# The blocks of an expert in turned order on odd steps, 64 slots for the expert of rank 24, and another pairing of the experts

## The chip, the cores and the metric

The kernel runs on one core of a Trainium2 chip. The core has five engines with a queue of instructions each: PE (TensorE, matrix multiplies), DVE (VectorE), ACT (ScalarE), POOL (GpSimd) and SP (SyncE, which starts transfers). The metric is the device time of one execution in microseconds; all times here are microseconds unless they are marked ns.

## The reference

One layer of a decoder for 1024 tokens of width 1024. Its last part, which the change touches, sends each token to 4 of 32 experts and adds up what these give, weighted:

```
act = clamped_swiglu(xb @ w_up[e] + b_up[e])     # w_up[e]: 1024 x 2048
return act @ w_down[e] + b_down[e]               # w_down[e]: 1024 x 1024
...
return jnp.zeros_like(h).at[slot_tok].add(ys * slot_gate[:, None].astype(ys.dtype))
```

Here `xb` are the tokens of one expert. The output of this part is added to its input and normalised. Ahead of it stand the projections, a sliding-window attention, a convolution branch, a layer norm and the router. All is float32.

## The kernel before, in words

The first 663 us are everything up to the router; then the experts run, and a short tail adds the result, normalises and stores it.

**Slots and blocks.** The experts are ranked by their number of tokens, and the one of rank j has `CAPS[j]` slots; what goes beyond them is done by a loop at the end, `overflow`, which runs no expert when all fit. The tokens of an expert are cut into blocks of 128, 64 or 32: 160 slots are 128 + 32, 320 are 128 + 128 + 64, 96 are 64 + 32. A block of 128 uses the whole array of PE; of 64 two column groups, of 32 four, with plain float32 matmuls. An expert with a block of 128 is `split`: each weight tile is cut into a high half (ACT, L87) and a low half (DVE, L88), and a 128-wide block takes three matmuls for each half of the outputs (L252). The narrower blocks use the weight tile as it came (L261).

**Steps and pairs.** An expert has 12 steps, each for one piece of weights: steps 0 to 3 make the first half of the up projection, 4 to 7 the second, 8 to 11 the down projection. In each step, `mm` runs over the expert's blocks, in rising order. Two experts make a pair (`PAIRS`, by rank) and take turns, four steps each; the pairs run one after the other, and the two experts of the last pair one after the other. Names in the trace begin with the rank: `p13l` is a low half of a weight tile of the expert of rank 13, `p13u` its accumulator of the up projection, `p13d` that of the down projection.

**What is issued around the matmuls.** Step numbers g run over the whole stage. A table, filled by `at(g, function, ...)`, says what is issued behind the matmuls of step g: the splits of weights, up to six halves ahead of the step that uses them; the transposes of a block's input (`x_T`); behind an expert's steps 3 and 7 the activation of all its blocks (`swiglus`, DVE L271 to L277 and ACT); the transposes of the activations (`act_T`); behind step 11 the evacuation of the result, scaled by the gates (`scale_out`, ACT L316); two steps later the scatter (`scatter`, POOL L320), an indirect transfer for each block that adds rows to `yd` in memory, one waiting for the landing of the one before. The bias of a 128-wide block comes by POOL: a row is loaded (L211), and broadcast to all partitions (`bias_of`, L226). Each engine runs its queue in the order of issue. There are five accumulators, handed out in the order in which they came free. The count of overflowing tokens, some 25 small operations on DVE, stands behind step 200.

Of the kernel before, what the change touches and what calls it, by code (L numbers as in the profile page):

```python
# [49 lines left out]
BROW, BC, ACTB, XG = 2, 3, 3, 3  # L50
V_AT, S_AT = (2, 3, 4, 5, 7), (0, 3)
CAPS = [320, 288, 256, 256, 256, 256, 192, 192, 192, 160, 160, 160, 160, 128, 128, 128,
        128, 128, 128, 96, 96, 96, 96, 96, 96, 64, 64, 64, 64, 64, 64, 64]
PAIRS = [(6, 31), (1, 30), (13, 19), (2, 29), (9, 14), (7, 20), (21, 22), (0, 28), (15, 23), (3, 27), (10, 16), (8, 24),
         (11, 17), (4, 26), (12, 18), (5, 25)]
TR = 9 * P
FDVE = (0, 4)

# [2 lines left out]
def kernel(ctx: ExitStack, tc: tile.TileContext, x, w_in, b_in, attn_sinks, w_attn_br,  # L61
# [33 lines left out]
    def acc(name):  # L95
        return ps.tile([P, 512], F32, name=name, tag="acc", bufs=5)
# [4 lines left out]
    class Expert:  # L101
# [130 lines left out]
        def mm(self, s, before=None):  # L232
            if s < 8 and s % 4 == 0 or s == 8:
                self.acc = [[acc(f"{self.pfx}{'d' if s == 8 else 'u'}{s}{i}{h}") for h in range(2 if w == P else 1)]
                            for i, (w, c) in enumerate(self.blocks)]
            raw, hi, lo = self.raw.pop(s), self.hi.pop(s, None), self.lo.pop(s, None)
            for i, (w, c) in enumerate(self.blocks):
                if before:
                    before(i)
                lhs = self.x[i] if s < 8 else self.aT[i]  # L240
                ng = P // w
                for kk in range(2):
                    k = 2 * (s % 4) + kk if s < 8 else 2 * (s - 8) + kk
                    st, sp = k == 0, k == KC - 1
                    if w == P and self.split:
                        terms = [(lhs[0], hi[kk]), (lhs[0], lo[kk]), (lhs[1], hi[kk])]
                    else:
                        terms = [(lhs[0], raw[kk])]
                    if w == P:
                        for h in range(2):  # L250
                            for j, (a, b) in enumerate(terms):
                                nc.tensor.matmul(self.acc[i][h], a[:, k, :], b[:, h * 512:(h + 1) * 512],  # L252
                                                 start=st and j == 0, stop=sp and j == len(terms) - 1)
                    else:
                        for j, (a, b) in enumerate(terms):
                            for g in range(ng):
                                if s < 8 and w == 32:
                                    rhs = b.rearrange("p (a f b t) -> p a b f t", a=2, b=2, t=2)[:, g // 2, g % 2]
                                else:
                                    rhs = b[:, g * 8 * w:(g + 1) * 8 * w]  # L260
                                nc.tensor.matmul(self.acc[i][0][g * w:(g + 1) * w, :8 * w], a[:, k, :], rhs,  # L261
                                                 start=st and j == 0, stop=sp and j == len(terms) - 1)
            wfree.extend(self.held.pop(s))
# [14 lines left out]
                                           op1=ALU.mult)  # L278

        def swiglus(self, v):  # L280
            for i, (w, c) in enumerate(self.blocks):
                for h in range(2 if w == P else 1):
                    self.swiglu(v, i, h)

# [41 lines left out]
    with ExitStack() as dctx:  # L326
# [391 lines left out]
        for b in range(NB + 1):  # L718
            i = 8 + b
# [119 lines left out]
        for c in range(KC):  # L839
            i = 38 + c  # L840
# [53 lines left out]
        for c in sorted(set(CAPS)):  # L894
            i, n = CAPS.index(c), CAPS.count(c)
# [198 lines left out]
        def expert_of(j):  # L1094
            ev = {}

            def value(eng=None):
                key = gated[0], eng
                if key not in ev:
                    src = (ids, ids2)[gated[0]]  # L1100
                    ev[key] = (eng or nc.sync).value_load(src[0:1, j:j + 1], min_val=0, max_val=NE - 1)
                return ev[key]

            return Expert(f"p{j}", CAPS[j], value, [t[:, j] for t in IDX])

        ex = [expert_of(j) for pair in PAIRS for j in pair]

# [71 lines left out]
    with tc.manual_schedule():  # L1179
# [173 lines left out]
        def at(g, f, *a):  # L1353
            todo.setdefault(g, []).append((f, a))
# [4 lines left out]
        for n, e in enumerate(ex):  # L1359
            p = g0[e.pfx] // 24 * 24  # L1360
            if n > 1:
                at(p - 16, e.fetch)
                at(p - 13, e.indices)
            for v in range(2):
                q = pos[e.pfx, 4 * v]
                at(q - 4, e.load_bias, v)
                at(q - 4, e.load_row, 2 * v)
                at(q - 3, e.load_row, 2 * v + 1)
                at(q, e.bias_of, 2 * v)
                at(q + 1, e.bias_of, 2 * v + 1)  # L1370
                at(q + 3, e.swiglus, v)
            for i in range(e.nb):
                at(pos[e.pfx, 4 + i], e.act_T, 0, i)
                at(pos[e.pfx, 8 + (i > 0)], e.act_T, 1, i)
                if e is not last:
                    at(pos[e.pfx, 11], e.scale_out, i)
            if e is not last:
                at(pos[e.pfx, 11] + (0 if e is ex[-2] else 2), e.scatter)
# [32 lines left out]
        e = ex[0]  # L1411
# [19 lines left out]
    with tc.If(nxv > 0):  # L1431
        last.scatter()
        with tc.For_i(0, nxv, 1) as it:
# [5 lines left out]
            e = Expert("x", P, lambda eng=nc.sync: ev[eng], idx, fast=False)  # L1439
# [48 lines left out]
```

## Time and profile before

| | |
|---|---|
| median of 3 runs | 2171.82 (2171.25 to 2172.2) |
| profiled execution | 2172.18, its span 2170.6 |
| busy: PE, DVE, ACT, POOL | 2065.7 (95%), 1373.6 (63%), 887.2 (41%), 487.9 (22%) |
| PE's granted clock, mean | 0.981 |
| moved by DMA | 508.74 MB, 234 GB/s |

Busy time of the engines overlaps, since they work beside each other; an engine with 95% bounds the kernel in most of the stretches, but not in each. The granted clock is a share of full speed.

### The profile page before, as it was taken

What the parts mean: (1) busy time and instruction counts of PE and PEld (TensorE: products, weight loads), DVE (VectorE), ACT (ScalarE), POOL (GpSimd) and SP (SyncE); (2) the same over time, 40 slices, a digit from 0 to 9 for tenths busy, and PEclk for the clock granted to TensorE, in tenths of its full rate; (3) what the DMA queues carried; (4) which work ended last, traced back from release to release, by engine and by line L of the source; (5) the groups of instructions that cost most, each with busy time, mean ns of one, the idle gap of its engine ahead of it and who ended that gap; (6) DMA issues with size and microseconds to landing.
All of it is one profiled execution on the core that took longest, in us unless ns stands there. A gap on an engine that the chain in (4) does not pass through costs nothing. (4 is left out here: it accounts for less than half of the span.)

```text
span 2170.6 us, 31922 instructions
## 1 busy us (share of the span) xinstructions
PE 2065.7 (95%) x10929; PEld 1368.4 (63%) x10929; DVE 1373.6 (63%) x2049; ACT 887.2 (41%) x1357; POOL 487.9 (22%) x649
## 2 busy tenths in 40 slices
PE   7999999998967999999999999999999999999993
PEld 6776788886744566566764346546766456767771
DVE  3768799666755545655965135465587559649755
ACT  3155511432333424444553122434366346446533
POOL 1000000004323221422322332133133332223111
PEclk9999999999988999999999999999999999999996
DMA  5111111142238988998898997799879988988985
GB/s 162 39 39 30 30 46 53 44 133 71 88 136 280 328 278 297 371 344 282 307 306 295 350 344 269 268 312 376 300 243 311 330 267 311 353 290 292 338 275 188
DMA packets 191302, 508.74 MB, mean 234 GB/s; under 512 B 34781, under 2 KB 71055, under 8 KB 191134
## 3 DMA queue, kind: packets, MB, share of 16 engines
q1 hardware_dynamic: 162342, 446.76, 58.0%
q0 software_dynamic: 28240, 58.23, 10.8%
q8 instruction: 87, 1.43, 0.3%
q10 hardware_dynamic: 551, 1.66, 0.2%
q14 instruction: 82, 0.66, 0.1%
HBM read 473.08 MB, written 33.49 MB: 233 GB/s over the span
## 5 line engine op out<-in xcount | busy, mean ns | idle before, releaser
L601 DVE SCALAR_TENSOR_TENSOR c<-a,cw,c 128x1024 f32<-128x1024 f32 x120 | 154.1, 1284 | 3.3
L829 POOL DMA_DIRECT2D bu<-in_b_up_dram x2 | 1.0, 502 | 450.8 <-DVE wol L88 450.8
L140 POOL DMA_DIRECT2D slt<-tab x103 | 54.4, 530 | 26.1 <-issue 12.9
L91 PE MATMUL ga<-xh,whga 128*128 128x512 f32 x128 | 52.1, 407 | 0.0
L93 PE MATMUL ga<-xh,wlga 128*128 128x512 f32 x128 | 50.5, 395 | 0.0
L92 PE MATMUL ga<-xl,whga 128*128 128x512 f32 x128 | 50.5, 394 | 0.0
L93 PE MATMUL gb<-xh,wlgb 128*128 128x512 f32 x128 | 50.4, 394 | 0.0
L91 PE MATMUL gb<-xh,whgb 128*128 128x512 f32 x128 | 50.4, 394 | 0.0
L92 PE MATMUL gb<-xl,whgb 128*128 128x512 f32 x128 | 50.4, 394 | 0.0
L1022 POOL DMA_INDIRECT tab<-rec,dst x32 | 32.4, 1011 | 59.5 <-DMA tab<-rec,dst 56.8
L928 PE MATMUL wo<-woh,mh 128*128 128x512 f32 x128 | 37.0, 422 | 0.6 <-ACT mh L87 0.6
L928 PE MATMUL wo<-woh,ml 128*128 128x512 f32 x128 | 35.9, 404 | 0.0
L88 DVE TENSOR_TENSOR p8l<-p8w,p8h 128x1024 fp32r<-128x1024 f32 x24 | 29.3, 1274 | 10.2 <-ACT p8h L87 6.1
L88 DVE TENSOR_TENSOR p7l<-p7w,p7h 128x1024 fp32r<-128x1024 f32 x24 | 29.5, 1279 | 9.7 <-ACT p7h L87 6.1
L442 ACT ACTIVATE gt<-ga,pcol 128x512 f32<-128x512 f32 x16 | 11.0, 691 | 59.2 <-PE ga L93 59.1
L88 DVE TENSOR_TENSOR p5l<-p5w,p5h 128x1024 fp32r<-128x1024 f32 x24 | 29.0, 1242 | 9.8 <-ACT p5h L87 9.2
L644 DVE SCALAR_TENSOR_TENSOR sc<-s,mask 128x512 f32<-128x512 f32 (+1 forms) x32 | 19.5, 652 | 23.9 <-PE s L641 21.8
L88 DVE TENSOR_TENSOR p0l<-p0w,p0h 128x1024 fp32r<-128x1024 f32 x24 | 29.5, 1266 | 7.5 <-ACT p0h L87 7.3
L928 PE MATMUL wo<-wol,mh 128*128 128x512 f32 x128 | 33.9, 399 | 0.0
L88 DVE TENSOR_TENSOR p11l<-p11w,p11h 128x1024 fp32r<-128x1024 f32 x24 | 29.3, 1275 | 4.8 <-ACT p11h L87 4.6
L88 DVE TENSOR_TENSOR p15l<-p15w,p15h 128x1024 fp32r<-128x1024 f32 x24 | 28.0, 1221 | 6.4 <-ACT p15h L87 6.1
L88 DVE TENSOR_TENSOR p1l<-p1w,p1h 128x1024 fp32r<-128x1024 f32 x24 | 28.5, 1240 | 5.0 <-ACT p1h L87 4.4
(1266 smaller groups left out, 6374.8 us busy)
## 6 DMA issues: line engine op xcount, KB each, us to landing
p6w<-in_w_up_dram SPq DMA_DIRECT2D x16, 512.0 KB
p31w<-in_w_up_dram SPq DMA_DIRECT2D x16, 512.0 KB
p1w<-in_w_up_dram SPq DMA_DIRECT2D x16, 512.0 KB
p30w<-in_w_up_dram SPq DMA_DIRECT2D x16, 512.0 KB
p13w<-in_w_up_dram SPq DMA_DIRECT2D x16, 512.0 KB
p19w<-in_w_up_dram SPq DMA_DIRECT2D x16, 512.0 KB
p2w<-in_w_up_dram SPq DMA_DIRECT2D x16, 512.0 KB
p29w<-in_w_up_dram SPq DMA_DIRECT2D x16, 512.0 KB
```

Source lines behind the costliest of these rows:

```text
L88: nc.vector.tensor_tensor(lo, src, hi.bitcast(F32), op=ALU.subtract)
L91: nc.tensor.matmul(o, ah, bh, start=start, stop=False)
L92: nc.tensor.matmul(o, ah, bl, start=False, stop=False)
L93: nc.tensor.matmul(o, al, bh, start=False, stop=stop)
L140: nc.gpsimd.dma_start(self.m[g * w:(g + 1) * w, i, :], tab[bass.ds(row + c, w), :])
L442: nc.scalar.activation(GT[c][:, sl], t, AF.Sigmoid, bias=bin_c(14 + c))
L601: nc.vector.scalar_tensor_tensor(C[c], A[c][:, w:w + S], cw[:, c, w:w + 1], C[c], op0=ALU.mult, op1=ALU.add)
L644: nc.vector.scalar_tensor_tensor(SC[b][c0 // 2][:, g::2, :W], t[g][:, :, :W], 0.125, mk[:, None, :].to_broadcast([P, 2, W]), op0=ALU.mult, ...
L829: nc.gpsimd.dma_start(bu, b_up[:, i * S:(i + 1) * S])
L928: nc.tensor.matmul(t, ml[:, k, :], W[k][:, sl], start=n == 0, stop=n == 3 * KC - 1)
L1022: nc.gpsimd.indirect_dma_start(out=tab[:, :], out_offset=bass.IndirectOffsetOnAxis(ap=DST[b][:, k:k + 1], axis=0), in_=REC[:, b, k, :], in ...
```

## The change

It has four parts: the expert of rank 24 has 64 slots instead of 96; the pairs are others; on odd steps `mm` runs over the blocks in falling order, so that the block that ended a step also begins the next; and the activations, the transposes of activations and the evacuations run over the blocks in falling order. The scatters keep the rising order.

```
 CAPS = [320, 288, 256, 256, 256, 256, 192, 192, 192, 160, 160, 160, 160, 128, 128, 128,
-        128, 128, 128, 96, 96, 96, 96, 96, 96, 64, 64, 64, 64, 64, 64, 64]
-PAIRS = [(6, 31), (1, 30), (13, 19), (2, 29), (9, 14), (7, 20), (21, 22), (0, 28), (15, 23), (3, 27), (10, 16), (8, 24),
-         (11, 17), (4, 26), (12, 18), (5, 25)]
+        128, 128, 128, 96, 96, 96, 96, 96, 64, 64, 64, 64, 64, 64, 64, 64]
+PAIRS = [(6, 31), (1, 30), (13, 14), (2, 29), (9, 19), (3, 28), (10, 20), (0, 27), (15, 16), (4, 26), (8, 23), (17, 18),
+         (11, 21), (7, 24), (12, 22), (5, 25)]
...
-            for i, (w, c) in enumerate(self.blocks):
+
+            for i in range(self.nb)[::-1 if s % 2 else 1]:
+                w, c = self.blocks[i]
...
         def swiglus(self, v):
-            for i, (w, c) in enumerate(self.blocks):
+            for i, (w, c) in reversed(list(enumerate(self.blocks))):
                 for h in range(2 if w == P else 1):
                     self.swiglu(v, i, h)
...
-            for i in range(e.nb):
+            for i in reversed(range(e.nb)):
                 at(pos[e.pfx, 4 + i], e.act_T, 0, i)
                 at(pos[e.pfx, 8 + (i > 0)], e.act_T, 1, i)
                 if e is not last:
```

Lines behind the change in `mm` have numbers that are higher by 2 in the changed kernel: L252 is L254, L261 is L263, L271 is L273, L316 is L318, L320 is L322.

**DVE at the start of the third pair.** That pair was (13, 19) and is (13, 14). What stands in DVE's queue around the first activation of expert 13 (`p13t`), before:

```order
L88 TENSOR_TENSOR p13l_6651<-p13w_6513,p13h_6650 128x1024
L88 TENSOR_TENSOR p13l_6694<-p13w_6515,p13h_6693 128x1024
L88 TENSOR_TENSOR p13l_6698<-p13w_6517,p13h_6697 128x1024
L271 TENSOR_TENSOR p13t_6780<-p13u_6654,p13bc_6683 128x512
L275 TENSOR_SCALAR p13t_6780<-p13t_6780 128x256
L276 SCALAR_TENSOR_TENSOR p13t_6780<-p13t_6780 128x256
L277 SCALAR_TENSOR_TENSOR p13act_6779<-p13sg_6782,p13t_6780 128x256
```

And in the changed kernel:

```order
L88 TENSOR_TENSOR p13l_6668<-p13w_6506,p13h_6667 128x1024
L88 TENSOR_TENSOR p13l_6672<-p13w_6508,p13h_6671 128x1024
L88 TENSOR_TENSOR p14xl_6692<-p14xt_6693,p14xh_6691 128x512
L88 TENSOR_TENSOR p14xl_6692<-p14xt_6700,p14xh_6691 128x512
L88 TENSOR_TENSOR p14l_6713<-p14w_6519,p14h_6712 128x1024
L88 TENSOR_TENSOR p14l_6717<-p14w_6521,p14h_6716 128x1024
L88 TENSOR_TENSOR p14l_6737<-p14w_6555,p14h_6736 128x1024
L88 TENSOR_TENSOR p14l_6741<-p14w_6557,p14h_6740 128x1024
L273 TENSOR_TENSOR p13t_6761<-p13u_6645,p13bc_6663 128x512
L277 TENSOR_SCALAR p13t_6761<-p13t_6761 128x256
L278 SCALAR_TENSOR_TENSOR p13t_6761<-p13t_6761 128x256
L279 SCALAR_TENSOR_TENSOR p13act_6760<-p13sg_6763,p13t_6761 128x256
```

The low halves of expert 14's input and of its first two steps have come to stand between expert 13's last halves of that phase and its activation; expert 19 needed none.

**ACT at the end of the second pair.** The evacuations of expert 1 (blocks 0 and 1 of 128, block 2 of 32 slots; `slt` holds the gates), before:

```order
L316 ACTIVATE p1ys0_6576<-p1d800_6360,slt_3627 128x512
L316 ACTIVATE p1ys0_6576<-p1d801_6361,slt_3627 128x512
L316 ACTIVATE p1ys1_6579<-p1d810_6362,slt_3627 128x512
L316 ACTIVATE p1ys1_6579<-p1d811_6363,slt_3627 128x512
L316 ACTIVATE p1ys2_6582<-p1d820_6364,slt_3627 128x256
```

And in the changed kernel:

```order
L318 ACTIVATE p1ys2_6567<-p1d820_6355,slt_3627 128x256
L318 ACTIVATE p1ys1_6569<-p1d810_6353,slt_3627 128x512
L318 ACTIVATE p1ys1_6569<-p1d811_6354,slt_3627 128x512
L318 ACTIVATE p1ys0_6572<-p1d800_6351,slt_3627 128x512
L318 ACTIVATE p1ys0_6572<-p1d801_6352,slt_3627 128x512
```

Block 0 has moved from the first place to the last. In POOL's queue of the changed kernel, where `gi` and `si` are the row numbers that a scatter writes to, these stand behind them:

```order
216 L211 DMA p13br0_6584<-bud128_69 1x16x32
217 L322 DMA yd_68<-p1ys0_6572,gi_3628 1152x1024
218 L322 DMA yd_68<-p1ys1_6569,gi_3628 1152x1024
219 L322 DMA yd_68<-p1ys2_6567,si_3629 4608x256
...
221 L211 DMA p13br1_6609<-bud128_69 1x16x32
222 L226 ISA p13bc0_6663<-p13br0_6584 128x512
...
225 L226 ISA p13bc1_6707<-p13br1_6609 128x512
```

Their order is that of the kernel before: the scatter of block 0 first, and the broadcasts of expert 13's two bias rows behind all three.

**PE between two steps of a 160-slot expert.** Expert 9, from the end of its step 0 to the beginning of its step 1, before (the numbers in the accumulators' names end in block and half):

```order
L252 MATMUL p9u001_8165<-p9h01_8134,p9xl0_8085 128x512
L261 MATMUL p9u010_8166<-p9w00_7946,p9xr1_8115 32x256 x4
L261 MATMUL p9u010_8166<-p9w01_7948,p9xr1_8115 32x256 x4
L252 MATMUL p9u000_8164<-p9h10_8142,p9xh0_8084 128x512
L252 MATMUL p9u000_8164<-p9l10_8143,p9xh0_8084 128x512
```

And in the changed kernel:

```order
L254 MATMUL p9u001_8251<-p9h01_8220,p9xl0_8169 128x512
L263 MATMUL p9u010_8252<-p9w00_8030,p9xr1_8201 32x256 x4
L263 MATMUL p9u010_8252<-p9w01_8032,p9xr1_8201 32x256 x4
L166 MATMUL p19xt00_8278<-ident_60,p19xg0_7947 128x64 x8
L263 MATMUL p9u010_8252<-p9w10_8073,p9xr1_8201 32x256 x4
L263 MATMUL p9u010_8252<-p9w11_8075,p9xr1_8201 32x256 x4
L254 MATMUL p9u000_8250<-p9h10_8228,p9xh0_8168 128x512
```

The narrow block of step 1 now follows that of step 0, here with transposes of the partner's input between them, and the 128-wide block comes behind it.

## Rows read from the trace of the kernel before

**Rows 1.** Windows by pair: PE, PEld, DVE, ACT, POOL busy; clock; DMA; GB/s

```profile
857.70:932.10 74.40, 74.15 (x480) 42.01 (x478) 47.92 (x68) 35.02 (x50) 25.96 (x36) 1.00 1.03 363
...
1024.90:1113.60 88.70, 86.65 (x524) 62.15 (x523) 81.39 (x104) 58.39 (x75) 27.00 (x35) 1.00 0.88 296
...
1403.80:1487.50 83.70, 77.48 (x484) 43.77 (x482) 53.10 (x103) 34.91 (x50) 25.20 (x35) 0.96 0.96 330
...
1580.30:1671.30 91.00, 88.20 (x525) 63.21 (x524) 81.04 (x104) 58.51 (x75) 34.92 (x36) 0.98 0.89 296
```

**Rows 2.** Timeline of PE: start, length; narrow blocks of ranks 30, 24, 11

```profile
854.13 3.65 PE L261 MATMUL p30d<-p30w,p30ar 128*64 128x512 f32 x16
...
1681.43 0.68 PE L166 MATMUL p24xt<-ident,p24xg 32*128 32x32 f32 x8
...
1691.65 11.67 PE L261 MATMUL p24u<-p24w,p24xr 128*64 128x512 f32 x96
...
1771.92 1.11 PE L261 MATMUL p11u<-p11w,p11xr 128*32 128x256 f32 x16
```

**Rows 3.** Timeline of PE: a 64-wide block of expert 8 between 128-wide ones

```profile
1716.03 0.39 PE L252 MATMUL p8u<-p8l,p8xh 128*128 128x512 f32 x1
1716.25 0.39 PE L252 MATMUL p8u<-p8h,p8xl 128*128 128x512 f32 x1
1716.57 1.94 PE L261 MATMUL p8u<-p8w,p8xr 128*64 128x512 f32 x8
1718.44 0.50 PE L252 MATMUL p8u<-p8h,p8xh 128*128 128x512 f32 x1
1718.78 0.40 PE L252 MATMUL p8u<-p8l,p8xh 128*128 128x512 f32 x1
```

**Rows 4.** Groups of PE, pair (10, 16), transposes: busy, mean ns, idle

```profile
L297 PE MATMUL p16aT<-ident,p16act 128*128 128x128 f32 x8 | 1.3, 281 | 0.0
...
L166 PE MATMUL p16xt<-ident,p16xg 128*128 128x128 f32 x8 | 1.1, 279 | 0.0
```

**Rows 5.** Timeline of DVE, start of pair (13, 19); in brackets idle, releaser

```profile
855.86 6.90 DVE L88 TENSOR_TENSOR p13l<-p13w,p13h 128x1024 fp32r<-128x1024 f32 x6
...
870.46 0.69 DVE L271 TENSOR_TENSOR p13t<-p13u,p13bc 128x512 f32<-128x512 f32 x1 [5.10 <-POOL p13bc L226]
...
876.26 0.69 DVE L271 TENSOR_TENSOR p13t<-p13u,p13bc 128x512 f32<-128x512 f32 x1 [3.78 <-POOL p13bc L226]
```

**Rows 6.** Timeline of POOL: first scatter of expert 1

```profile
846.30 1.67 POOL L320 DMA_INDIRECT yd<-p1ys,gi  x1 [21.15 <-ACT p1ys L316]
```

**Rows 7.** Timeline of ACT: evacuations of expert 1

```profile
844.63 1.38 ACT L316 ACTIVATE p1ys<-p1d,slt 128x512 f32<-128x512 f32 x2 [8.10 <-PE p1d L252]
...
849.07 0.47 ACT L316 ACTIVATE p1ys<-p1d,slt 128x256 f32<-128x256 f32 x1 [0.34 <-PE p1d L261]
```

**Rows 8.** Timeline of DVE, pair (10, 16)

```profile
1601.94 4.63 DVE L88 TENSOR_TENSOR p16l<-p16w,p16h 128x1024 fp32r<-128x1024 f32 x4 [0.41 <-ACT p16h L87]
...
1648.20 0.69 DVE L88 TENSOR_TENSOR p10al<-p10aT,p10ah 128x512 fp32r<-128x512 f32 x1
```

**Rows 9.** Timeline of DVE, pair (15, 23): overflow count, its first, what follows

```profile
1435.29 0.18 DVE L1231 TENSOR_TENSOR over<-scnt_ps,capr 128x32 f32<-128x32 f32 x1
...
1441.74 0.69 DVE L88 TENSOR_TENSOR p15al<-p15aT,p15ah 128x512 fp32r<-128x512 f32 x1
```

**Rows 10.** Timeline of PE, pair (15, 23): a matmul behind a gap

```profile
1443.61 0.79 PE L252 MATMUL p15u<-p15l,p15xh 128*128 128x512 f32 x1 [5.39 <-DVE p15l L88]
```

**Rows 11.** Timeline of all engines: end of expert 5 and the gather behind it

```profile
2104.25 1.37 ACT L316 ACTIVATE p5ys<-p5d,slt 128x512 f32<-128x512 f32 x2 [6.93 <-PE p5d L252]
2105.91 1.69 POOL L320 DMA_INDIRECT yd<-p5ys,gi  x1 [19.00 <-ACT p5ys L316]
...
2106.97 1.37 ACT L316 ACTIVATE p5ys<-p5d,slt 128x512 f32<-128x512 f32 x2 [1.35 <-PE p5d L252]
...
2123.19 1.02 POOL L1287 DMA_INDIRECT yg<-yd,si  x1 [3.74 <-DMA yd<-p5ys,gi]
```

## The prediction

> **What bounds the kernel now.** I first cut the trace into stretches of one pair each, from one pair's first matmul to the next pair's [rows 1]. The four pairs of a 160-slot and a 128-slot expert and the pair of 128 and 96 slots show two kinds of bound. In all of them PE is busy nearly throughout; in the 160+128 pairs DVE is busy too, 81 to 82 of 89 to 91 us, since every 128-wide block makes it form the low half of each weight tile. In pairs with one such expert DVE is busy about 50 us. So the expert stage is bound by PE, with DVE close behind wherever two split experts meet. The last 40 us are a chain of scatter, load, statistics and output.
>
> **What PE no longer does: 14.5 us.** Expert 24 loses its 32-wide block. Four of its steps (64 + 32) take 11.67, two steps of a 64-slot expert 3.65, so four take 7.2 [rows 2]: 4.5 in each of three phases, 13.5; then eight transposes of its input, 0.68, and two of its activations, estimated at 0.3 from those. In the reference's draw that expert (25th by its count) has 57 tokens, so 64 slots hold them and the overflow loop stays empty; had it more than 64, that loop would run a whole expert for it.
>
> **Changes of form: 12 us.** Turning the order on odd steps makes blocks of one width neighbours across a step's end. Counted in PE's listing, the expert matmuls change between 128-, 64- and 32-wide 382 times before and 241 times after. Of the 141, 21 are expert 24's own, counted above; 120 are left. The price, from one 64-wide block between two 128-wide ones [rows 3]: matmuls follow each other by 0.23, the last before the change takes 0.32, the first after the block 0.34, and the block 1.87 against 1.82 alone [rows 2]. That is 0.09 + 0.05 + 0.11 for a change there and one back, some 0.12 each; 0.09 if only one side pays, 0.17 if the last matmul of the narrow block waits too. A third of the places have transposes between the steps, which change the form anyway, so I take 0.10: 12 us, bounds 11 and 20. [...]
>
> **Old stalls that go: 24 us.** A 128-wide block's step is 12 x 0.23 = 2.74, and one with a 32-wide block 2.74 + 1.11 + 0.15 = 4.0 [rows 2, 3]. A 160+128 pair needs 12 x (4.0 + 2.74) = 81. Its transposes take 1.1 for the input and 1.3 for the activations of each 128-wide block [rows 4], with the narrow block and the changes of form around them about 5: 86. The four such pairs took 88.7 to 91.0 [rows 1], the two not shown 88.9 and 88.7: 3, 5, 3, 3 lost. The 128+96 pair (15, 23) needs 74 and took 83.7: 10. After the change the 160-slot experts run with 96-slot ones, which need no split. Bounds: 15 (the idle time of PE alone in [rows 1]) and 26.
>
> **New stalls: three pairs of two 128-slot experts, 55.6 us.** The change makes (13, 14), (15, 16) and (17, 18). Such a pair needs 24 x 2.74 = 65.8 on PE, and the same 5.1 of transposes: 70.9. DVE is its bound, worked out in the queue's own order from t = 0 at the first matmul:
> 1. Now DVE starts p13's low halves at -1.8 (855.86 against 857.7), 1.15 each, and has eight by 7.7, where it goes idle [rows 5]. After the change the next things in its queue are p14's input (1.4) and four of p14's halves (4.6): 13.7. Only then comes p13's first swiglu.
> 2. That swiglu needs two bias rows broadcast by POOL, and POOL sends them behind the three scatters of the wide expert just done. Now DVE gets the first at 870.46 (12.8) and the second at 876.26 (18.6) [rows 5]. The scatters go in the order 0, 1, 2 before and after, and the first starts when block 0 is evacuated [rows 6]. Turned, block 0 is the last of p1's step 11, so its evacuation is where block 2's is now, 849.07 for 844.63 [rows 7]: 4.4 later for the whole chain. DVE waits from 13.7 to 17.2, adds and scales for 2.0 (870.46 to 876.26, less the 3.78 idle), waits from 19.2 to 23.0, and ends at 25.0: 7.3 us of idle DVE.
> 3. Behind it stand the halves of p14's third step, done at 27.2. PE had come there at 4 x 2.74 + 1.1 + 2 x 2.74 = 17.5 (p13's four steps, p14's transposes, p14's first two): a gap of 9.7.
> 4. From there DVE runs without a break, as in (10, 16) from the end of the first swiglu, 1601.53, to the low half of the second activations, 1648.89 [rows 8]: 47.4, less about 1.3 for that pair's 32-wide block: 46. So PE's 19th step starts at 71.2, and the other six with their transposes take 19: 90.3, that is 19.4 lost.
> (15, 16) follows the 320-slot expert, so the same, plus the overflow count, which stands on DVE in that pair for 6.4 [rows 9] with nothing left to hide it: 25.8. (17, 18) follows (8, 23): two scatters only, biases in time, and 96-wide steps before it, so DVE starts 2 earlier; its first swiglu ends at 16.1, and 46 + 0.2 + 19 later it is over: 81.3, 10.4 lost. Sum 55.6. Bounds: 38 if POOL's rows come in time and DVE runs 1 faster per pair; 65 if every gap also costs 3 of half-speed time that nothing absorbs.
>
> **Tail: 2.7 us.** Expert 5's blocks are turned in step 11 too. Its first scatter starts with block 0's evacuation, 2105.91, the two evacuations are 2.72 apart, and the gather behind the scatters waits for their landing [rows 11]. Block 0 now comes second, so all of it moves by 2.7 (0 if the second scatter alone decides).
>
> **At no cost.** The turned swiglus free the narrow block's accumulator first, which the next expert then takes, so no matmul waits there; each would be some 2 us, six times, if the accumulator were block 0's. The turned lists of transposes and evacuations issue the same instructions. The loads are as many as before, six to nine steps ahead in the listing. In mixed experts a 3.9 us longer wait for block 0's swiglu is hidden by the partner's four steps (7.2 at least).
>
> **Sum.** The profiled execution took 2172.18 (span 2170.6), the median of three runs 2171.82, 0.4 less. 2172.2 - 14.5 - 12 - 24 + 55.6 + 2.7 = 2180.0; as a median, **2179.6**.
>
> **Rivals.**
> - The biases come in time (POOL's chain is not moved, or lands faster): 7.3 less in two pairs, 2165. For it: the chain's steps of 10 us are landings, and vary. Against: the first scatter waits for the evacuation in [rows 6]. It decides from 4 us of change per pair on.
> - DVE stays ahead, and the three pairs lose no more than today's worst ones, 3 + 10 + 3 = 16: 40 less, 2140, faster. For it: 160+128 pairs carry the same splits. Against: their PE time is 86 for DVE's 81; here 70.9 for about 78 (81 less the narrow block's share).
> - A change of form is worth 0.17: 8 less (120 x 0.07), 2171.2, no change. [...]
> [...]
>
> **Chances.** Forecast as summed 0.44, clock 0.12, changes dear 0.14, biases in time 0.19, DVE ahead 0.11. A measurement tells 0.2% (4.3 us) from no change. Slower: the clock and most of the forecast, 0.48. Same: dear changes, a third of biases in time, a little of the forecast, 0.25. Faster: the rest, 0.27. The range takes in biases in time together with dear changes (2157) and leaves out the case at 2140 and the far end of the clock: 2157 to 2192; the likeliest case alone spans 2171 to 2188.
>
> **What will show it.** In the profile after: (13, 14) and (15, 16) some 90 and 97 long with DVE busy over 80%, (17, 18) some 81; a gap of PE before p14u's third step with p14l as its releaser, 8 to 11 us; DVE's p13t waiting for POOL's p13bc; no waits left in pairs 9 to 12; expert 24's four steps at 7.2. Wrong if these pairs last under 80, or if PE's busy time falls by more than 35.

## The result

The changed kernel took 2195.7 us (median of 4 runs, 2195.11 to 2197.3), the kernel before 2171.53 beside it (4 runs, 2167.48 to 2172.2): a ratio of 1.0112, with a 95% interval of 1.01 to 1.0123. The direction was forecast, and the size was not: 24 slower for 8, and 3.7 above the upper end of the range. The profiled execution took 2195.11, its span 2193.0; PE was busy for 2054.7 of it (94%), DVE for 1371.8 (63%), and the mean granted clock was 0.97.

The windows by pair of the changed kernel, with the columns of [rows 1]; they are (13, 14), (9, 19), (15, 16), (17, 18) and (7, 24):

```profile
857.50:945.70 88.20, 76.47 (x330) 60.92 (x329) 80.09 (x96) 57.67 (x72) 30.07 (x32) 0.92 0.91 307
1038.40:1125.20 86.80, 86.80 (x674) 47.67 (x672) 50.10 (x76) 36.55 (x54) 25.62 (x36) 1.00 0.99 339
1422.10:1518.80 96.70, 79.54 (x334) 63.85 (x333) 85.45 (x130) 57.88 (x72) 28.43 (x32) 0.89 0.85 281
1707.80:1791.00 83.20, 75.85 (x331) 59.96 (x329) 77.27 (x94) 56.18 (x69) 32.69 (x42) 0.96 0.94 315
1877.50:1960.50 83.00, 83.00 (x378) 42.99 (x376) 44.56 (x64) 32.89 (x46) 29.14 (x37) 1.00 0.93 332
```

The three pairs of two 128-slot experts last 88.2, 96.7 and 83.2; the forecast was some 90, 97 and 81. In the other two PE is busy from the first to the last microsecond. So the three pairs and the others went nearly as worked out. The larger miss is in no pair.

The last output leaves at 2176.45 in the changed kernel and at 2165.13 in the one before, 11.3 later, where the forecast was 7.8; the span grew by 22.4.

```profile
2176.45 1.04 POOL L1346 DMA_INDIRECT out_dram<-yg,si  x1 [36.56 <-DVE yg L1343]
```

```profile
2165.13 1.04 POOL L1344 DMA_INDIRECT out_dram<-yg,si  x1 [34.76 <-DVE yg L1341]
```

The other 11.1 lie behind the last output, where no engine is counted as busy. Windows from the last output to the end of the span, first of the changed kernel, then of the one before:

```profile
2176.40:2193.00 16.60, 0.00 (x0) 0.00 (x0) 0.00 (x0) 0.00 (x0) 1.04 (x1) 0.50 0.04 16
```

```profile
2165.10:2170.60 5.50, 0.00 (x0) 0.00 (x0) 0.00 (x0) 0.00 (x0) 1.04 (x1) 0.50 0.13 49
```

That is 16.6 for 5.5. What fills most of it are instructions of POOL's sequencer (POOLq); the view of a single source line shows them: the line that opens the program, to which its closing instructions are put down, and the line of the branch around the overflow loop. Columns: count, then shortest, median and longest duration in ns, and when the first and the last began. The changed kernel:

```profile
L1486 POOLq DRAIN  x3: 56/109/9872, 2182.0 to 2192.4; - x3
...
L1433 POOLq INC_SWDGE_SEM  x1: 2597/2597/2597, 2179.4 to 2179.4; - x1
```

And the kernel before:

```profile
L1484 POOLq DRAIN  x3: 56/109/1127, 2168.6 to 2170.3; - x3
...
L1431 POOLq INC_SWDGE_SEM  x1: 451/451/451, 2168.1 to 2168.1; - x1
```

One DRAIN takes 9.87 for 1.13, and the INC_SWDGE_SEM ahead of it 2.60 for 0.45: 10.9 of the 11.1. No term of the prediction stands for this.

### The profile page after: what moved, and what is told of

Its sections match the earlier page's. It is cut to its first block, busy times and chain, and to the rows that moved or that the text cites. A ratio compares the mean times of both kernels' runs of the same rounds, so it can differ in the third digit from the quotient of the medians.

```text
span 2193.0 us, 31430 instructions
## 1 busy us (share of the span) xinstructions
PE 2054.7 (94%) x10727; PEld 1380.4 (63%) x10727; DVE 1371.8 (63%) x2040; ACT 886.3 (40%) x1351; POOL 473.1 (22%) x635
## 4 chain that ended last, share of the span: by engine, by line
PE 75%; issue 12%; DVE 6%; DMA 3%; ACT 1%; POOL 1%; POOLq 0%; DVEq 0%; ACTq 0%
PE wo L930 4%; PE p3u L254 2%; PE p4u L254 2%; PE p2u L254 2%; PE p0u L254 2%; PE ga L91 1%; PE ga L93 1%; PE gb L91 1%; PE gb L93 1%; PE gb L92 1%; PE ga L92 1%; PE p12u L254 1%; PE p10u L254 1%; PE p9u L254 1%; PE p8u L254 1%
## 5 line engine op out<-in xcount | busy, mean ns | idle before, releaser
L831 POOL DMA_DIRECT2D bu<-in_b_up_dram x2 | 1.0, 500 | 451.9 <-DVE wol L88 451.9
L140 POOL DMA_DIRECT2D slt<-tab x99 | 52.5, 532 | 23.3 <-issue 15.8
L88 DVE TENSOR_TENSOR p9l<-p9w,p9h 128x1024 fp32r<-128x1024 f32 x24 | 28.9, 1251 | 11.7 <-ACT p9h L87 11.7
L88 DVE TENSOR_TENSOR p8l<-p8w,p8h 128x1024 fp32r<-128x1024 f32 x24 | 28.5, 1241 | 11.3 <-ACT p8h L87 11.3
L88 DVE TENSOR_TENSOR p10l<-p10w,p10h 128x1024 fp32r<-128x1024 f32 x24 | 29.0, 1254 | 9.6 <-ACT p10h L87 9.4
L88 DVE TENSOR_TENSOR p12l<-p12w,p12h 128x1024 fp32r<-128x1024 f32 x24 | 28.4, 1241 | 9.2 <-ACT p12h L87 9.2
## 6 DMA issues: line engine op xcount, KB each, us to landing
p31w<-in_w_up_dram SPq DMA_DIRECT2D x16, 512.0 KB, 10.9
```

Source lines behind the costliest of these rows:

```text
L88: nc.vector.tensor_tensor(lo, src, hi.bitcast(F32), op=ALU.subtract)
L140: nc.gpsimd.dma_start(self.m[g * w:(g + 1) * w, i, :], tab[bass.ds(row + c, w), :])
L831: nc.gpsimd.dma_start(bu, b_up[:, i * S:(i + 1) * S])
```

## The experiments

The question of the first four is which part of the change brings what, and with which part the long end comes.

**The pairs alone.** The edit is the change's own list of pairs in the kernel before.

```
-PAIRS = [(6, 31), (1, 30), (13, 19), (2, 29), (9, 14), ...
+PAIRS = [(6, 31), (1, 30), (13, 14), (2, 29), (9, 19), ...
```

> The kernel before with the new pairs alone (rising block order, 96 slots for rank 24). Theory A, the prediction's sum: -24 for the stalls that go, +55.6 for the three 128+128 pairs, less 4.4 in each of two of them because without the turn the first scatter is not late: +23, 2194 against 2171.5. Theory B: the 11 us that the changed kernel spent behind its last output (16.6 from the last POOL transfer to the end of the span, 5.5 before) belong to the pairs: 2205. Rival: the 128+128 pairs cost less without the turn than DVE's queue says, under 2185.

Measured: 2200.19, ratio 1.0137 (1.0123 to 1.0152). The end is short (DRAIN 1.13), so it does not come with the pairs, and theory B falls. The time is 6 above theory A. The three pairs last 90.1, 93.2 and 83.6; the rival, that they cost little without the turn, falls too. What was 6 too cheap is (13, 14): it was to be 4.4 shorter than with the turn, and is 1.9 longer. The 1.9 itself means little, since this pair lasts 88.2, 88.8, 91.1 and 91.2 in four executions with the turn (the changed kernel and the three with something added on POOL, below). (15, 16) is 3.5 shorter, near the 4.4.

**The turn alone.** The edit is the turned order of the change, in `mm`, in the activations and in their transposes and evacuations, with the old slots and pairs.

```
-            for i, (w, c) in enumerate(self.blocks):
+            for i in range(self.nb)[::-1 if s % 2 else 1]:
+                w, c = self.blocks[i]
...
-            for i, (w, c) in enumerate(self.blocks):
+            for i, (w, c) in reversed(list(enumerate(self.blocks))):
...
-            for i in range(e.nb):
+            for i in reversed(range(e.nb)):
```

> The kernel before with the turned block order alone (old pairs, 96 slots). Theory A: 120 changes of form at 0.10 less, 2.7 more in the tail: 2171.5 - 12 + 2.7 = 2162, the last POOL transfer to the end of the span 5.5. Theory B: the 11 us at the end come with the turn: 2173. Rival, from the pairs that stand in both traces ((1, 30) 106.6 and 106.4, (2, 29) 92.8 and 92.6, (4, 26) 92.6 and 92.6): a change of form is worth 0.03 or less, and the turn gives nothing but the later scatter, 2171 to 2174.

Measured: 2171.49, ratio 1.0 (0.9992 to 1.0009); the end is short (DRAIN 1.13). That is the rival's time, though not quite its reason. The windows of (13, 19) and (15, 23), 74.4 and 83.7 in [rows 1]:

```profile
859.60:937.30 77.70, 75.92 (x481) 43.48 (x479) 47.96 (x67) 34.61 (x49) 27.41 (x36) 0.98 1.00 346
1407.10:1492.30 85.20, 77.01 (x485) 43.98 (x483) 53.33 (x102) 34.54 (x49) 26.77 (x36) 0.96 0.93 318
```

These two got 3.3 and 1.5 longer and the last pair 2.0, and the others 8.5 shorter together. Some 2 of these need not be a gain of the turn: pair (10, 16) lasts 91.0 in the trace of the kernel before, but 88.6 in the next run, where nothing of it is changed. So the changes of form do bring something, and the later scatters take most of it back. The expert stage as a whole began 2.9 later in this execution, behind a part that the edit does not touch, so a few us between two kernels are better read from the lengths of pairs.

**The 64 slots alone.**

```
-        128, 128, 128, 96, 96, 96, 96, 96, 96, 64, 64, 64, 64, 64, 64, 64]
+        128, 128, 128, 96, 96, 96, 96, 96, 64, 64, 64, 64, 64, 64, 64, 64]
```

> The kernel before with 64 slots for rank 24 alone. Theory A: 14.5 less, 2157, pair (8, 24) 83 long for 97.7, the end as before. Theory B: the 11 us at the end come with the smaller number of POOL's instructions, since expert 24 then has fewer transfers: 2168.

Measured: 2169.88, ratio 0.9998 (0.9989 to 1.0007). The pair (8, 24), before and with 64 slots:

```profile
1671.30:1769.00 97.70, 97.70 (x580) 47.75 (x578) 49.38 (x72) 36.25 (x53) 29.71 (x41) 1.00 0.94 308
```

```profile
1668.70:1752.00 83.30, 83.30 (x377) 42.50 (x375) 43.31 (x62) 33.04 (x47) 22.36 (x29) 1.00 1.00 345
```

14.4 are saved there, as forecast, and the kernel is no faster beyond the noise: it ends with a DRAIN of 9.87 and an INC_SWDGE_SEM of 2.61.

```profile
L1484 POOLq DRAIN  x3: 52/257/9872, 2156.2 to 2167.2; - x3
```

The long end belongs to the 64 slots, theory B. Some 3 should be left of the gain: the spans of the two profiled executions differ by 3.2, the medians by 0.5, and the interval reaches only to 2.4. What took the rest in the medians is open.

**Turn and 64 slots, the old pairs.** The edit is the change without its list of pairs.

> The changed kernel with the old pairs. Theory A: 2171.5 - 14.5 - 12 + 2.7 = 2148. Rival, changes of form worth nearly nothing: 2157 to 2160. Theory B, the 11 us at the end come with the turn or with the 64 slots and not with the pairs: 2159 to 2171, and 16 us from the last POOL transfer to the end of the span.

Measured: 2166.43, ratio 0.9977 (0.9967 to 0.9987), DRAIN 9.87: theory B again. The pairs (13, 19) and (15, 23) last 79.2 and 87.6, in a profiled execution of 2171.36, the slowest of eleven.

```profile
856.30:935.50 79.20, 76.00 (x481) 43.53 (x479) 47.36 (x67) 34.58 (x49) 27.70 (x36) 0.98 1.00 342
1405.40:1493.00 87.60, 77.65 (x485) 44.26 (x483) 53.22 (x102) 34.56 (x49) 26.83 (x36) 0.96 0.92 311
```

The next three ask what of the 64 slots makes the end long. Expert 24's narrow block takes with it, besides its matmuls, POOL's transfers for it: a gather, a scatter, four loads of its slots and eight of its biases, 14 in all. Counted in the program, POOL issues 497 transfers ahead of the branch in the kernel before, and 483 in the changed one. Each of the three adds something to the changed kernel, ahead of the loads of the up bias, where POOL is idle for 451.9; each of the three was run once.

**Six transfers more.**

```
+        dum = const.tile([1, 8], F32, name="dum")
+        for _ in range(6):
+            nc.gpsimd.dma_start(dum, ln1_g[0:1, 0:8])
         for i in range(2):
             load_up_bias(i)
```

> The changed kernel with 6 small transfers more on POOL ahead of the up bias, where POOL is idle for 450 us (489 of POOL's transfers ahead of the branch at the end; 483 in the changed kernel, 497 in the kernel before; the last transfer then uses the same of the eight semaphores as in the kernel before). Theory C, the long end of the program hangs on which of the semaphores the last transfers use: the final DRAIN takes about 1.1 for 9.9, and the time falls by 11, to 2185. Theory D, it hangs on the total of POOL's transfers, or Theory E, on the number of POOL's instructions: 9.9 and 2196.

Measured: 2200.24 in the one run, with the end longer still:

```profile
L1489 POOLq DRAIN  x3: 52/109/10509, 2186.9 to 2198.0; - x3
...
L1436 POOLq INC_SWDGE_SEM  x1: 2717/2717/2717, 2183.9 to 2183.9; - x1
```

Theory C falls. The two instructions grew by 0.76 of the 4.5. Most of the rest is in the pairs: (13, 14), (15, 16) and (17, 18) last 91.1, 97.6 and 84.2 here for 88.2, 96.7 and 83.2. In the next run (13, 14) lasts 91.2; whether the added transfers do this or it varies so by itself, these single runs do not tell.

**Fourteen transfers more.** The same edit with `range(14)`.

> The changed kernel with 14 such transfers more: 497, as many as in the kernel before. Theories C and D: the final DRAIN takes about 1.1, and the time is 2185. Theory E (number of instructions, here some 16 to 42 more): 9.9 unless the count happens to fit.

Measured: 2184.05, 11.65 less than the changed kernel:

```profile
L1489 POOLq DRAIN  x3: 52/109/1127, 2180.1 to 2181.8; - x3
...
L1436 POOLq INC_SWDGE_SEM  x1: 460/460/460, 2179.6 to 2179.6; - x1
```

Fourteen transfers that do nothing make the kernel some 11 us faster, in one run. Each of them brings 8 numbers, far less than the transfers of expert 24 that they stand for, and the two instructions take what they take in the kernel before within 0.01 (1.13 for 1.13 and 0.46 for 0.45): in these runs their length goes by the number of transfers, 497 in both, and not by the bytes.

**As many instructions, no transfer.**

```
+        for _ in range(43):
+            nc.gpsimd.memset(dum, 0.0)
```

> The changed kernel with 43 small memsets more on POOL and no transfer, so that POOL issues 1699 instructions as in the kernel before. Theory E: the final DRAIN takes about 1.1, and the time is 2185. Theories C and D: 9.9 and 2196.

Measured: 2195.53, DRAIN 9.87, INC_SWDGE_SEM 2.61.

```profile
L1489 POOLq DRAIN  x3: 52/109/9872, 2182.7 to 2193.2; - x3
```

Theory E falls; of what was tried, the number of transfers decides.

**The kernel before with 40 transfers more.** The same edit with `range(40)`; this one had to forecast a length that no run had shown.

> The kernel before with 40 small transfers more on POOL at the same place: 537. Theory D in its finer form (the INC_SWDGE_SEM and the final DRAIN take time by the number of transfers since a point between the 490th and the 497th; from 483 to 489 transfers the DRAIN grew by 0.64, so 0.106 each): the DRAIN takes 1.1 + 4.3 = 5.4, and the time is 2171 + 5 = 2176. Rival: the end has two lengths only, so 1.1 and 2171, or 9.9 and 2182.

Measured: 2174.64, in one run.

```profile
L1487 POOLq DRAIN  x3: 52/109/4400, 2167.8 to 2172.8; - x3
...
L1434 POOLq INC_SWDGE_SEM  x1: 1266/1266/1266, 2166.5 to 2166.5; - x1
```

The DRAIN takes 4.4 for 5.4: the length does grow with the number, by (4.40 - 1.13) / 40 = 0.08 for each transfer if it does not fall in between, and the rival of two lengths falls.

The last four concern the bias rows, and a kernel faster than both.

**Scatters in falling order.**

```
-            for i, (w, c) in enumerate(self.blocks):
+            for i, (w, c) in reversed(list(enumerate(self.blocks))):
                 nc.gpsimd.indirect_dma_start(out=yd.rearrange("t (c d) -> (t c) d", c=P // w),
```

> The changed kernel with the scatters in falling order of blocks, the order in which the evacuations now come. Theory A: the first scatter starts 4.4 earlier behind expert 1 and some 5 earlier behind expert 0, so DVE no longer waits 6.3 and 7.2 for the bias rows in pairs (13, 14) and (15, 16) but 2 to 3; these pairs get some 4 shorter each, and the tail 2.7: 2196 - 10.7 = 2185. Rival, the bias wait is slack that the splits' own pace takes back: only the tail, 2193. The end of the program stays at 16.6.

Measured: 2190.27, ratio to the kernel before 1.0085 (1.0068 to 1.0102), so 5.4 less than the changed kernel: half of theory A, and more than its rival. Pair (13, 14) lasts 85.7 for 88.2, (15, 16) 93.2 for 96.7, and the last pair with the tail 144.2 for 145.7. DVE still waits 3.7 in (13, 14) for the bias rows; the broadcast of the first takes 4.94 of POOL here, where it takes 1.23 in the changed kernel.

**Bias rows four steps earlier.**

```
-BROW, BC, ACTB, XG = 2, 3, 3, 3
+BROW, BC, ACTB, XG = 2, 4, 3, 3
...
-                at(q - 4, e.load_row, 2 * v)
-                at(q - 3, e.load_row, 2 * v + 1)
-                at(q, e.bias_of, 2 * v)
-                at(q + 1, e.bias_of, 2 * v + 1)
+                at(q - 8, e.load_row, 2 * v)
+                at(q - 7, e.load_row, 2 * v + 1)
+                at(q - 4, e.bias_of, 2 * v)
+                at(q - 3, e.bias_of, 2 * v + 1)
```

> The changed kernel with the bias rows of 128-wide blocks loaded and broadcast four steps earlier, so that they stand ahead of the three scatters in POOL's queue, and with four buffers for them instead of three. Theory A: DVE's first activation no longer waits; pair (13, 14) falls by 6.3 from 88.2 to 82, (15, 16) by 7.2 from 96.7 to 89.5, and the time to 2182. Rival: the waits are slack that the pace of the splits takes back; the pairs stay within 2, and the time is 2193 or more.

Measured: 2183.76, ratio 1.0062 (1.0045 to 1.0079). The windows of (13, 14), (15, 16) and (17, 18):

```profile
854.80:938.60 83.80, 75.85 (x330) 60.39 (x329) 80.10 (x96) 57.77 (x72) 27.30 (x29) 0.96 0.98 332
1415.00:1505.00 90.00, 76.79 (x334) 60.81 (x333) 85.54 (x131) 57.69 (x72) 28.66 (x29) 0.94 0.91 306
1694.00:1775.00 81.00, 73.95 (x330) 58.84 (x329) 77.25 (x94) 56.03 (x69) 39.98 (x42) 0.98 0.95 321
```

These are 4.4, 6.7 and 2.2 less, in a profiled execution of 2178.31, the fastest of four; (17, 18) had no wait for a bias row to lose. DVE's first activation of (13, 14) follows its low halves without a wait. By the medians the kernel is 11.9 faster than the changed one, for 13.5 of waits: the bias wait is real, and most of it shows in the time, theory A.

**The parts put together.** Turn and 64 slots with the old pairs, the scatters in falling order, and 14 transfers more.

> The turned order and the 64 slots with the old pairs, the scatters in falling order, and 14 small transfers more on POOL. From 2166.4 with turn and 64 slots alone: 11 less for the end of the program, 2.7 for the tail, 3 to 4 each in pairs (13, 19) and (15, 23), where the turn had delayed the bias rows: 2145 to 2149. If the scatters' order is worth only the tail: 2153.

Measured: 2147.11, ratio 0.9899 (0.9881 to 0.9917). Pairs (13, 19) and (15, 23) last 73.5 and 81.7; with the scatters in rising order they took 77.7 and 85.2 (the turn alone) and 79.2 and 87.6 (with the 64 slots). The DRAIN takes 1.13.

```profile
855.70:929.20 73.50, 73.46 (x480) 42.45 (x478) 47.55 (x67) 33.94 (x49) 25.29 (x35) 1.00 1.03 352
1397.40:1479.10 81.70, 76.08 (x484) 43.98 (x482) 53.25 (x102) 34.65 (x50) 24.91 (x36) 0.96 0.98 327
```

**The same with the bias rows earlier.**

> The same as e11 with the bias rows four steps earlier as in e10. Theory A: what is left of the bias waits in (13, 19) and (15, 23) goes, another 3 to 8: 2138 to 2145. Rival, the overflow count and the splits set these pairs: within 2 of e11.

Measured: 2145.23, ratio 0.9885 (0.9868 to 0.9901). The two pairs last 73.6 and 82.0: the rival. With the falling scatters DVE still waited 3.6 and 3.7 for a bias row in them, and now it does not wait for one; but in (13, 19) PE was busy for 73.46 of 73.50 already, and in (15, 23) what PE waits for is one low half, 5.6 and then 5.2. So the waits that were left cost nothing.

## Why the prediction was wrong

**The step that failed** is "What PE no longer does: 14.5 us". The gain it worked out is there (14.4 in the 64 slots' own run), but it counted what leaves PE and not what leaves POOL. Fourteen of POOL's transfers go with the narrow block, and by their number the program's end grew from 5.5 to 16.6. The sum starts from the profiled execution and has no term for its end; "At no cost" names the loads and not POOL's transfers. So the end was put at no change without a reason. None of the prediction's signs of being wrong came, since they look at the pairs and at PE: the shortest of the three pairs lasts 83.2, and PE's busy time fell by 11.0. Without these 11.1 the changed kernel would have taken 2184.6, inside the range and 5 above the forecast; the one run with 14 transfers more, 2184.05, is that kernel.

**Changes of form: 12 us.** That fewer of them save time was right, the size was not. (9, 19) and (8, 23) stand in the run with the pairs alone in rising order and in the changed kernel turned, with 18 and 15 changes of form less: 88.0 against 86.8, 97.3 against 96.3.

```profile
1039.20:1127.20 88.00, 88.00 (x674) 46.65 (x672) 49.98 (x76) 36.79 (x54) 28.51 (x37) 1.00 0.98 326
...
1611.30:1708.60 97.30, 97.30 (x573) 47.30 (x571) 50.49 (x73) 36.42 (x52) 25.72 (x32) 1.00 0.89 295
```

That is 2.2 for 33, or 0.067 each where 0.10 was taken and 0.09 was held to be the least: some 8 for all 120. The neighbourhood in [rows 3] was read as the price everywhere. The rival of 0.17 is out.

**Old stalls that go: 24 us.** The mechanism was right: in the changed kernel's pairs of 160 and 96 slots PE is busy throughout (86.80 of 86.80 in the first, and likewise in the other three). The size can be had from the run with the pairs alone: its expert stage, up to the last pair, is 27.5 longer than before (1403.5 for 1376.0), and its three pairs have 54.2 over 70.9 each, so some 26.7 have gone elsewhere, just above the upper bound.

**New stalls: 55.6 us.** Measured against 70.9 each: 17.3 + 25.8 + 12.3 = 55.4. The sum is that close by luck, since 2.1 less in (13, 14) and 1.9 more in (17, 18) cancel. DVE's timeline at the start of (13, 14), where [rows 5] showed the kernel before:

```profile
855.68 9.17 DVE L88 TENSOR_TENSOR p13l<-p13w,p13h 128x1024 fp32r<-128x1024 f32 x8
864.77 1.28 DVE L88 TENSOR_TENSOR p14xl<-p14xt,p14xh 128x512 fp32r<-128x512 f32 x2
865.97 4.62 DVE L88 TENSOR_TENSOR p14l<-p14w,p14h 128x1024 fp32r<-128x1024 f32 x4
873.30 0.69 DVE L273 TENSOR_TENSOR p13t<-p13u,p13bc 128x512 f32<-128x512 f32 x1 [2.71 <-POOL p13bc L226]
...
878.89 0.69 DVE L273 TENSOR_TENSOR p13t<-p13u,p13bc 128x512 f32<-128x512 f32 x1 [3.57 <-POOL p13bc L226]
```

The pair begins at 857.5. DVE has done p14's first halves at 13.1 (13.7 was worked out), gets the bias rows at 15.8 and 21.4 (17.2 and 23.0), waits 6.3 in all (7.3), and is through with the activation at 24.4 (25.0). And PE, at p14's third step:

```profile
881.04 0.80 PE L254 MATMUL p14u<-p14h,p14xh 128*128 128x512 f32 x1 [6.00 <-ACT p14h L87]
883.08 0.79 PE L254 MATMUL p14u<-p14l,p14xh 128*128 128x512 f32 x1 [1.24 <-DVE p14l L88]
```

PE came there 17.5 behind the start, as worked out (881.04 less 6.00), and waited for 6.0 and 1.2 where one gap of 9.7 with DVE as its releaser was forecast. The first wait's releaser is ACT and not DVE: ACT's high halves of that step stand behind the sigmoids of the same activation, the last of them at 879.62 and the halves from 879.95 on. The two matmuls took 0.80 and 0.79 where the one ahead of the gap took 0.39; the granted clock was 0.50 from 881 to 887.5 and 1.00 from 888 to 893, and from 883.08 to 887.84 eleven matmuls took 4.76, where eleven at the 0.23 by which they follow each other elsewhere take 2.5. The pairs' granted clock is 0.92, 0.89 and 0.96, but the sum of their lengths is that of DVE's queue within 0.2 without a term for the clock. That DVE absorbs it is argued from this and not shown by a run. In (15, 16) the overflow count shows as forecast: behind it PE waits 5.84 for `p15l`.

```profile
1472.27 0.79 PE L254 MATMUL p15u<-p15l,p15xh 128*128 128x512 f32 x1 [5.84 <-DVE p15l L88]
```

From there to 1478.33 fourteen matmuls took 6.06 for 3.2, at a granted clock of 0.50 (1472.3 to 1478). No run shows the 3 us of half-speed time for a gap, which are in the upper bound of 65, nor a loss by the clock, which has 0.12 of the chances: what the trace shows in their place is 2.2 and 2.8 more on PE behind these two gaps.

**Step 2 inside it**, "4.4 later for the whole chain", held in (15, 16): there DVE waits 7.2 for the bias rows in the changed kernel and 2.1 with the pairs alone. It did not hold in (13, 14), and other delays took its place. With the pairs alone the first scatter starts early, and the bias row comes just as late, 15.8 behind the pair's start (872.30 against 856.5). POOL with the pairs alone:

```profile
845.10 1.66 POOL L320 DMA_INDIRECT yd<-p1ys,gi  x1 [22.30 <-ACT p1ys L316]
855.43 1.90 POOL L320 DMA_INDIRECT yd<-p1ys,gi  x1 [8.67 <-ACT p13h L87]
866.66 4.33 POOL L320 DMA_INDIRECT yd<-p1ys,si  x1 [9.34 <-ACT p14h L87]
871.03 1.24 POOL L226 PARTITION_BROADCAST p13bc<-p13br  x1
```

And in the changed kernel:

```profile
849.82 1.65 POOL L322 DMA_INDIRECT yd<-p1ys,gi  x1 [26.35 <-ACT p1ys L318]
859.74 2.00 POOL L322 DMA_INDIRECT yd<-p1ys,gi  x1 [8.26 <-DMA yd<-p1ys,gi]
868.39 3.62 POOL L322 DMA_INDIRECT yd<-p1ys,si  x1 [6.64 <-DMA yd<-p1ys,gi]
...
872.04 1.23 POOL L226 PARTITION_BROADCAST p13bc<-p13br  x1
```

The first scatter starts 4.7 earlier with the pairs alone, and the third ends only 1.0 earlier, as much as the pair begins earlier. Of the 3.7 lost, 2.6 lie between the starts of the second and the third (11.2 for 8.7), 0.4 between those of the first and the second, and 0.7 in the third's own time on POOL. The third's wait is put down to the second's landing in the changed kernel (6.64) and to ACT's `p14h` with the pairs alone (9.34). Why it took longer there, no run shows.

That own time goes with DVE's low halves in these traces. Of the 103 scatters in the traces of the kernel before and the changed one, 75 take 1.55 to 1.71 of POOL. The other 28 take 1.79 to 3.62, and each of them ends 1.4 to 1.6 behind the end of one of DVE's low halves. For most it is the first that ends behind the scatter's start: the second scatter here ends at 861.74 in the changed kernel, 1.43 behind a low half, while DVE goes on with the next. The third misses such ends, one in the changed kernel and two with the pairs alone, and gets through 1.4 behind the last: 872.01 against 870.59, 871.00 against 869.57. That a stretched scatter waits for a low half to end is the author's reading of these times; why the third misses an end that the second catches is open, and no run took DVE's low halves away to show the cause.

In pair (13, 19) of the kernel before the third scatter, at 867.62, falls into DVE's idle time of 5.10 [rows 5] and takes 1.55. In the old pairs the turned scatters do cost time: 77.7 and 85.2 with the turn alone, against 73.5 and 81.7 in falling order.

**Tail: 2.7 us.** In the changed kernel the first scatter of expert 5 starts 69.9 behind the pair's start (2117.26 against 2047.4), in the one before 66.7 (2105.91 against 2039.2): 3.2.

```profile
2117.26 1.70 POOL L322 DMA_INDIRECT yd<-p5ys,gi  x1 [21.71 <-ACT p5ys L318]
```

The terms as the runs give them, -14.4 - 8 - 26.7 + 55.4 + 3.2 + 11.1, make 20.6; the spans differ by 22.4. The 8 is extended from two pairs, and the stage of the changed kernel began 0.9 later, behind a part that the change leaves as it was.

## What to carry to other kernels

Where an edit removes transfers from POOL's queue or adds some, look behind the last output, from there to the end of the span (16.6 for 5.5 here): the view of engines shows nothing there, and the sequencer's own instructions have to be asked for by their line. A part that gains 14 where it was aimed and nothing in the time has given it back somewhere else; its own run, read up to the end of the span, shows where. A pair of experts that fits PE has to fit DVE too: in (13, 14) DVE was busy for 80.1 of 88.2, and PE for 76.5. DVE's queue could be worked out here from rows of the kernel before, to some 2 us in each of the three pairs.

## What had not been expected of the hardware

The closing INC_SWDGE_SEM and DRAIN of POOL took, by the number of POOL's transfers ahead of them: 483, 2.60 to 2.61 and 9.87 (the changed kernel, the 64 slots alone, the turn with 64 slots, and the 43 memsets); 489, 2.72 and 10.51; 497, 0.45 to 0.46 and 1.13 (the kernel before, the pairs alone, the turn alone, the fourteen transfers, and the parts put together); 537, 1.27 and 4.40. From 483 to 489 and from 497 to 537 they grow: INC_SWDGE_SEM by 0.02 for a transfer in both stretches, DRAIN by 0.11 and 0.08. From 489 to 497 they fall, by 2.26 and 9.38. At 0.02 for each, the fall of INC_SWDGE_SEM is the growth of some 110 transfers; this is an estimate, and 110 times 0.08 comes near the 9.38 of the DRAIN. Why they fall there, and whether they do so at other numbers, no run shows.
